# A fused decoder block: the first weight block's low half on VectorE, ScalarE and VectorE in another order in the head, and four powers of the queries' norms behind the state-space units on GpSimd

## The chip, the core and the metric

One Trainium2 chip, one core of it. The metric is the device time of one execution in microseconds (us), lower is better. The kernel is one program with five engines, each of which works through its own instruction list in order: TensorE (PE; its weight loads are counted apart as PEld), VectorE (DVE), ScalarE (ACT), GpSimd (POOL) and SyncE (SP, which here only issues transfers).

## The reference

One decoder layer over 512 tokens of width 1024, all float32, with three token mixers side by side: a sparse attention that picks its keys with an indexer (DSA), an attention with compressed, selected and windowed keys (NSA), and a state-space mixer in chunks of 128 tokens (SSD).

```python
h = rms_norm(x, g1)
u = h @ W_in                      # 1024 x D_in, split among the three mixers and three gates
y_A = DSA(u_A) @ W_br_A
y_B = NSA(u_B) @ W_br_B           # its queries are RMS-normed per head of 64
y_C = SSD(u_C) @ W_br_C
x = x + (sig(g_A)*y_A + sig(g_B)*y_B + sig(g_C)*y_C) @ W_out
x = x + relu(rms_norm(x, g2) @ W_1)**2 @ W_2

def rms_norm(x, g):
    return x * lax.rsqrt(jnp.mean(x*x, axis=-1, keepdims=True) + EPS) * g
```

## The kernel before, in words

**Products.** Each float32 product is made of three matmuls on numbers split into a high and a low part: `whi`·`hTh` (L459), `wlo`·`hTh` (L460) and `whi`·`hTl` (L461). `hTh` and `hTl` are the split, normed and transposed input; `whi` and `wlo` the split weights.

**The weight stream.** An object `ws` loads raw blocks of weights (`wraw`, three buffers, issued by SP) and splits them: ScalarE copies the high part (L173), then the difference is the low part (L175), on VectorE, or on GpSimd for the blocks whose number is in the set `LOWP`. Before the change, block 0 is in that set.

**The head.** The 512 tokens are four blocks of 128, x0 to x3 (in the lists of instructions x0 is `x_121`, x1 `x_124`, x2 `x_125`, x3 `x_126`). x0 takes a path of its own: it is transposed, multiplied by the gain `g1c` per column (`xg`, L406, two halves), then by `rb` (L432), the reciprocal root of each token laid along a row by a small matmul on `dg` (L416), and split into `hTh` (ScalarE, L433) and `hTl` (VectorE, L434). The blocks x1 to x3 are squared and summed on ScalarE (L394, L396), get a root on GpSimd (a power, L410), are scaled in place by VectorE (two L413 of 512 columns each), transposed by TensorE into `pT` (L428, eight 128x128 for each block), and split by ScalarE (`hTh`, L438) and VectorE (`hTl`, L439). `pT` has two buffers of four transposes each, so that the transposes of one block need the buffers that the block ahead of it left: both its `hTh` and its `hTl` must have read them. The first projection, 96 matmuls of 456 columns, goes over four weight blocks (0 to 3), two column halves of each and the four token blocks.

Small constants are loaded on SP between the weight blocks: `gq_d`, `gk_d`, `gk_n` (L324, read by VectorE in L344 and L345) and, later, `dsk` (read in L357 into `dcol`).

**The state-space mixer** runs through the middle of the kernel, its units woven between the matmuls of later projections. For each unit GpSimd masks `E` (L1345), ScalarE takes exponentials of it (L1348), VectorE multiplies (L1355), TensorE multiplies with `xt` and `hst`, VectorE and GpSimd combine (`eab`, L1366, L1367), and the result is gated and squared (`zsl` and `yv`, L1387 to L1404).

**The NSA queries** lie as raw rows; the sums of squares of each head are in `ssn`. Four powers on GpSimd (L1812, one for each token block) make the reciprocal roots in `rs8`. Then GpSimd issues the loads of the queries back from memory (`qu`, L1046), and TensorE makes the scores (L1087).

**What sets the order.** The program is written in Python, and a scheduler with a model of the engines' timelines orders the instructions of all engines, each engine's list fixed when the kernel is built. `tc.high_priority(...)` raises a group, `with tc.issue_after(X):` lets an instruction be placed only after X. So an edit at one place can reorder others. Semaphores hold an instruction until what it reads is written, and until buffers that it writes are free.

Of the kernel before, what the change touches and what calls it, by code (L numbers as in the profile page):

```python
# [10 lines left out]
ALU = mybir.AluOpType  # L11
# [12 lines left out]
NS = 6  # L24
RAWB = 3
LEAD = 3
LOWP = {0} | set(range(8, 12)) | set(range(17, 24))
WE = 2
NH = 4
BH = 2  # L30
# [6 lines left out]
HB = {4: 2, 5: 3}  # L37
# [4 lines left out]
def build_kernel(ctx, tc, A, out):  # L42
    nc = tc.nc
    pe, act, dve, pool = nc.tensor, nc.scalar, nc.vector, nc.gpsimd
# [5 lines left out]
    def bc(ap, shape):  # L50
        return ap.to_broadcast(shape)
# [63 lines left out]
    xt = []  # L115
# [18 lines left out]
    class WS:  # L134
# [24 lines left out]
        def split(s):  # L159
            i = s.nsplit  # L160
            while s.nload <= i:
                s.load()
            _, n, w = s.specs[i]
            r = s.raw.pop(i)
            m = n * w
            after = None
            if callable(r):
                after = r.after
                r = r(False)
            hi = wp.tile([128, 1024], F32R, name="whi", tag="whi", bufs=NS)  # L170
            lo = wp.tile([128, 1024], F32R, name="wlo", tag="wlo", bufs=NS)
            with tc.issue_after(HX[HB[i]][0]) if i in HB else nullcontext():
                act.activation(hi[:, :m], r[:, :m], AF.Copy)  # L173
            with tc.issue_after(H0[0][1]) if i == 1 else nullcontext():
                (pool if i in LOWP else dve).tensor_tensor(lo[:, :m], r[:, :m], f(hi[:, :m]), op=ALU.subtract)  # L175
            s.hl[i] = (hi[:, :m].rearrange("p (a b) -> p a b", b=w), lo[:, :m].rearrange("p (a b) -> p a b", b=w))
            s.nsplit += 1
            if after is not None:
                after()
# [123 lines left out]
    for t in range(NB):  # L303
        if t:
            nc.sync.dma_start(xt[t], dram(A["x"], t * 128 * D, [[D, 128], [1, D]]))
        if t == 2:
            ws.split()
        for _ in range((2, 1, 1, 0)[t]):
            ws.load()

# [62 lines left out]
    sq_junk = x0.tile([128, D], mybir.dt.bfloat16, name="sq_junk")  # L373
    ss1 = cp.tile([128, NB], F32, name="ss1")
    rs1 = cp.tile([128, NB], F32, name="rs1")
    H0, XG, g1p = [], [], []
    HX = {}
    wm = ps("pv", [128, 512])

    def warm(n, ref=None):  # L380
        with tc.issue_after(getattr(ref, "ins", ref)) if ref is not None else nullcontext():
            for _ in range(n):
                pe.matmul(wm[:, 0:128], ident, ident, start=True, stop=True)
# [6 lines left out]
    for t in range(NB):  # L390
        with tc.high_priority(offset=0 if t else HP):
            if t == 1:
                with tc.issue_after(H0[0][0]):
                    act.activation(sq_junk, xt[t], AF.Square, accum_out=ss1[:, t:t + 1])  # L394
            elif t:
                act.activation(sq_junk, xt[t], AF.Square, accum_out=ss1[:, t:t + 1])  # L396
            else:
                act.activation(sq_junk[:, 0:512], xt[0][:, 0:512], AF.Square, accum_out=ssh[:, 0:1])
                dve.tensor_tensor_reduce(xg, xt[0][:, 512:], xt[0][:, 512:], 1.0, 0.0, ALU.mult, ALU.add, accum_out=ssh[:, 1:2])
                dve.tensor_tensor(ss1[:, 0:1], ssh[:, 0:1], ssh[:, 1:2], op=ALU.add)  # L400
                for k0 in range(0, KT, 4):
                    p = ps("pT", [128, 4, 128])
                    for k in range(4):
                        i_ = pe.transpose(p[:, k], xt[t][:, (k0 + k) * 128:(k0 + k + 1) * 128], ident)
                    xg_ = x0.tile([128, 4, 128], F32, name=f"xg{k0}")
                    dve.tensor_tensor(xg_, p, bc(g1c[:, k0:k0 + 4, None], [128, 4, 128]), op=ALU.mult)  # L406
                    XG.append(xg_)
                warm(WARM[1], i_)
            dve.tensor_scalar(ss1[:, t:t + 1], ss1[:, t:t + 1], 1.0 / D, EPS, op0=ALU.mult, op1=ALU.add)
            pool.tensor_tensor(rs1[:, t:t + 1], ss1[:, t:t + 1], mhalf[:, :1], op=ALU.pow)  # L410
            if t:
                for i, c in enumerate((0, 512)):
                    dve.scalar_tensor_tensor(xt[t][:, c:c + 512], xt[t][:, c:c + 512], rs1[:, t:t + 1], g1p[i], op0=ALU.mult, op1=ALU.mult)  # L413
            else:
                dg = x0.tile([128, 128], F32, name="dg")
                dve.tensor_scalar(dg, ident, rs1[:, 0:1], None, op0=ALU.mult)  # L416
                rb = ps("pF", [128, 512])[:, 0:128]
                i_ = pe.matmul(rb, ones, dg, start=True, stop=True)
                for c in (0, 512):
                    p = ps("sc", [128, 512])  # L420
                    with tc.issue_after(getattr(i_, "ins", i_)):
                        pe.matmul(p, one1, g1w[:, c:c + 512], start=True, stop=True)
                    g1p.append(p)
            for k0 in range(0, KT, 4):
                if t:
                    p = ps("pT", [128, 4, 128])
                    for k in range(4):
                        pe.transpose(p[:, k], xt[t][:, (k0 + k) * 128:(k0 + k + 1) * 128], ident)  # L428
                else:
                    hsl = (slice(None), slice(k0, k0 + 4), slice(0, 128))  # L430
                    xg_ = XG[k0 // 4]
                    dve.tensor_tensor(xg_, xg_, bc(rb[:, None, :], [128, 4, 128]), op=ALU.mult)  # L432
                    h0 = act.activation(hTh[hsl], xg_, AF.Copy)  # L433
                    l0 = dve.tensor_tensor(hTl[hsl], xg_, f(hTh[hsl]), op=ALU.subtract)  # L434
                    H0.append([getattr(i, "ins", i) for i in (h0, l0)])
                    continue
                hsl = (slice(None), slice(k0, k0 + 4), slice(t * 128, t * 128 + 128))
                i_ = act.activation(hTh[hsl], p, AF.Copy)  # L438
                l_ = dve.tensor_tensor(hTl[hsl], p, f(hTh[hsl]), op=ALU.subtract)  # L439
                HX[t] = [getattr(v, "ins", v) for v in (i_, l_)]  # L440
# [436 lines left out]
            defer(1, tr)  # L877


    MASK = {}  # L880
    RIDX = R0

# [424 lines left out]
    def ssd(sv, ratio):  # L1307
# [50 lines left out]
        def stage3(u):  # L1358
            g, c = u.g, u.c
            py = ps("sc", [128, 512])  # L1360
            if c:
                po = ps("sc", [128, 512])
                for k in range(4):
                    mm(po[:, 128 * k:128 * k + 128], hst[g][:, 128 * k:128 * k + 128], u.b[:, 1])
                t1 = u.ea.rearrange("p k i -> p (k i)")
                dve.tensor_tensor(t1, po, t1, op=ALU.mult)  # L1366
                pool.tensor_tensor(t1, t1, u.xd, op=ALU.add)  # L1367
                yield ratio * 960
            if c < 3:
                pst = ps("pT", [128, 512])  # L1370
# [420 lines left out]
    def main():  # L1791
# [17 lines left out]
        yield "nq"  # L1809
        dve.tensor_scalar(ssn, ssn, 1.0, 64 * EPS, op0=ALU.mult, op1=ALU.add)  # L1810
        for b in dict.fromkeys(b for b, _ in NORD):
            pool.tensor_tensor(rs8[:, b, 16:32], ssn[:, b], mhalf[:, :16], op=ALU.pow)  # L1812
        at = popen("att", side="right")
        tail()
        yield from pipeline(nsa_units(R2), R2)
# [64 lines left out]
```

## Time and profile before

| | |
|---|---|
| runs | 1347.91, 1351.69, 1347.1 us, median 1347.91 |
| the profiled execution, its own time | 1345.58 us |
| its span (first to last instruction) | 1343.9 us |
| TensorE busy | 1326.1 us, 99% |
| VectorE, ScalarE, GpSimd busy | 994.2, 729.3, 266.8 us |
| mean granted TensorE clock | 0.997 |

The busy times are those of the one profiled execution and are shares of its span; 1.7 us of its time lie outside the span. Engines overlap, so their times don't add up to it. Matmuls are pipelined: a matmul's row gives more than its spacing (0.37 us for a spacing of 0.21 in the head).

### The profile page before, as it was taken

How to read it: one execution, taken by the hardware profiler on the slowest of the kernel's cores; microseconds unless marked ns; L12 is line 12 of the kernel's file. 1: busy time of each engine (PE TensorE's matmuls, PEld its weight loads, DVE VectorE, ACT ScalarE, POOL GpSimd, SP SyncE). 2: the span in 40 equal slices, each digit the busy share in tenths (PEclk: the TensorE clock that was granted, in tenths of full speed). 3: DMA queues.
4: the chain of work that ended last, by engine and by line, in shares of the span. 5: the costliest groups of instructions: out<-in, count | busy, mean ns of one | idle time of the engine just before them, and what ended most of it. 6: DMA issues, size and time to landing. Idle time of an engine off the chain costs nothing.

```text
span 1343.9 us, 19617 instructions
## 1 busy us (share of the span) xinstructions
PE 1326.1 (99%) x6827; PEld 1106.5 (82%) x6827; DVE 994.2 (74%) x1979; ACT 729.3 (54%) x1395; POOL 266.8 (20%) x236
## 2 busy tenths in 40 slices
PE   9999999999999999999999999999999999999998
PEld 7888788888887867888888888878889888888887
DVE  6499986889969576677687799978654766757841
ACT  5455336677768765565666656565343443444520
POOL 2225111111017677300000023213000201102000
PEclk9999999999999999999999999999999999999999
DMA  6436664464469899743344555334526646746431
GB/s 201 122 92 168 189 180 122 129 171 130 139 211 352 267 300 291 214 128 106 113 126 143 161 148 155 125 124 147 180 81 187 137 146 140 180 116 125 146 124 47
DMA packets 251777, 213.74 MB, mean 159 GB/s; under 512 B 15881, under 2 KB 203165, under 8 KB 251678
## 3 DMA queue, kind: packets, MB, share of 16 engines
q1 hardware_dynamic: 235708, 188.88, 46.5%
q0 software_dynamic: 15232, 20.98, 8.3%
q10 hardware_dynamic: 738, 2.63, 0.6%
q8 instruction: 54, 0.88, 0.3%
q14 instruction: 45, 0.37, 0.1%
HBM read 171.75 MB, written 40.70 MB: 158 GB/s over the span
## 4 chain that ended last, share of the span: by engine, by line
PE 82%; DVE 9%; DMA 4%; issue 2%; ACT 1%; POOL 1%; SPq 0%; DVEq 0%; POOLq 0%; ACTq 0%
PE pj L459 19%; PE pj L460 19%; PE pj L461 19%; PE sc L459 4%; PE sc L460 4%; PE sc L461 4%; PE pT L987 3%; PE pv L1000 2%; PE pv L999 2%; PE sc L927 2%; PE sc L928 2%; PE sc L1315 1%; DMA wraw<-in_w_in_dram 1%; DVE wlo L175 1%; DVE mask L904 1%
## 5 line engine op out<-in xcount | busy, mean ns | idle before, releaser
L173 ACT ACTIVATE whi<-wraw 128x1024 fp32r<-128x1024 f32 (+2 forms) x190 | 198.6, 1047 | 248.8 <-PE pj L460 123.7
L175 DVE TENSOR_TENSOR wlo<-wraw,whi 128x1024 fp32r<-128x1024 f32 (+1 forms) x178 | 222.8, 1254 | 99.5 <-ACT whi L173 98.7
L459 PE MATMUL pj<-hTh,whi 128*128 128x512 f32 x512 | 203.2, 397 | 4.4 <-DVE zo L736 2.3
L460 PE MATMUL pj<-hTl,whi 128*128 128x512 f32 x512 | 202.4, 395 | 0.0
L461 PE MATMUL pj<-hTh,wlo 128*128 128x512 f32 x512 | 202.1, 395 | 0.0
L936 ACT ACTIVATE p<-p,nb,rs 128x384 f32<-128x384 f32 (+3 forms) x160 | 107.8, 677 | 40.2 <-DVE nb L934 37.3
L459 PEld LDWEIGHTS pj<-hTh,whi 128*128 128x128 f32 x512 | 96.3, 188 | 23.6 <-DVE zo L736 2.7
L461 PEld LDWEIGHTS pj<-hTh,wlo 128*128 128x128 f32 x512 | 96.2, 188 | 19.0 <-issue 0.2
L460 PEld LDWEIGHTS pj<-hTl,whi 128*128 128x128 f32 x512 | 96.3, 188 | 18.2 <-issue 0.3
L460 PE MATMUL pj<-h2l,whi 128*128 128x512 f32 (+1 forms) x256 | 96.3, 376 | 0.0
L461 PE MATMUL pj<-h2h,wlo 128*128 128x512 f32 (+1 forms) x256 | 96.2, 376 | 0.0
L459 PE MATMUL pj<-h2h,whi 128*128 128x512 f32 (+1 forms) x256 | 96.1, 376 | 0.0
L459 PE MATMUL pj<-whi,hTh 128*128 128x512 f32 (+2 forms) x208 | 81.1, 390 | 0.6 <-ACT hTh L433 0.6
L461 PE MATMUL pj<-whi,hTl 128*128 128x512 f32 (+2 forms) x208 | 81.0, 389 | 0.0
L1046 POOL DMA_DIRECT2D qu<-q_d x32 | 23.5, 736 | 287.3 <-PE sc L928 121.3
L460 PE MATMUL pj<-wlo,hTh 128*128 128x512 f32 (+2 forms) x208 | 80.4, 387 | 0.0
L991 ACT ACTIVATE pth<-pT 128x512 fp32r<-128x512 f32 x92 | 53.1, 594 | 30.8 <-PE pT L987 29.9
L459 PE MATMUL sc<-whi,fh 128*128 128x512 f32 x168 | 65.4, 389 | 0.0
L460 PE MATMUL sc<-wlo,fh 128*128 128x512 f32 x168 | 65.4, 389 | 0.0
L461 PE MATMUL sc<-whi,fo 128*128 128x512 f32 x168 | 65.2, 389 | 0.0
L992 DVE TENSOR_TENSOR ptl<-pT,pth 128x512 fp32r<-128x512 f32 x92 | 61.6, 679 | 2.4 <-ACT pth L991 2.4
L987 PE MATMUL pT<-ident,p 128*128 128x128 f32 x368 | 63.1, 272 | 0.0
(431 smaller groups left out, 3275.5 us busy)
## 6 DMA issues: line engine op xcount, KB each, us to landing
wraw<-in_w_in_dram SPq DMA_DIRECT2D x84, 512.0 KB, 4.1
wraw<-in_w_ff_dram SPq DMA_DIRECT2D x58, 512.0 KB, 4.0
qd<-in_w_ff_dram POOLq DMA_DIRECT2D x18, 512.0 KB, 5.9
gld<-g_d SPq DMA_DIRECT2D x35, 256.0 KB, 2.6
q_d<-qev SPq DMA_DIRECT2D x64, 128.0 KB, 3.3
qu<-q_d POOLq DMA_DIRECT2D x32, 256.0 KB, 3.6
E<-ac_d SPq DMA_DIRECT2D x16, 512.0 KB, 6.1
xz<-xzt_d SPq DMA_DIRECT2D x16, 512.0 KB, 5.6
```

The lines of the kernel that those rows point to most:

```text
L173: act.activation(hi[:, :m], r[:, :m], AF.Copy)
L175: (pool if i in LOWP else dve).tensor_tensor(lo[:, :m], r[:, :m], f(hi[:, :m]), op=ALU.subtract)
L459: pe.matmul(o, lh, rh, start=first, stop=False)
L460: pe.matmul(o, lh, rl, start=False, stop=False)
L461: pe.matmul(o, ll, rh, start=False, stop=last)
L927: pe.matmul(s_[:, h % w, :n], u.q[h], kh[:, :n], start=True, stop=False)
L928: pe.matmul(s_[:, h % w, :n], u.q[h], kl[:, :n], start=False, stop=True)
L936: act.activation(u.p[h][:, :n], u.p[h][:, :n], AF.Exp, bias=u.nb[:, h:h + 1], scale=rs8[:, u.b, u.h0 + h:u.h0 + h + 1], accum_out=u.sm[:, ...
L987: pe.transpose(pt[:, h], u.p[h][:, kb * 128:kb * 128 + 128], ident)
L991: act.activation(ph, ptf, AF.Copy)
L992: dve.tensor_tensor(pl, ptf, f(ph), op=ALU.subtract)
L999: pe.matmul(o, vk, ph0, start=st, stop=False)
```

## The change

It has two parts.

In the head: block 0 leaves `LOWP`, so its low part goes to VectorE; the split of block 0 is issued after the first `xg`·`rb` rather than while x is loaded; VectorE's order is fixed as the first `xg`, then `dg`, and the low part of block 0 after the first multiplication by `rb`; ScalarE splits block 1 after the first `hTh` and block 2 after the second, and squares x1 after the second; the scaling of x1 (L413) comes after the second `hTl`.

In the middle: the four powers L1812 come after the last `eab` addition (L1367) of the state-space units.

```diff
-LOWP = {0} | set(range(8, 12)) | set(range(17, 24))
+LOWP = set(range(8, 12)) | set(range(17, 24))
...
-            with tc.issue_after(HX[HB[i]][0]) if i in HB else nullcontext():
+            with tc.issue_after(H0[0][0] if i == 1 else H0[1][0] if i == 2 else HX[HB[i]][0]) if i in (1, 2) or i in HB else nullcontext():
                 act.activation(hi[:, :m], r[:, :m], AF.Copy)
-            with tc.issue_after(H0[0][1]) if i == 1 else nullcontext():
+            with tc.issue_after(H0[0][1] if i else GX[2]) if i < 2 else nullcontext():
                 (pool if i in LOWP else dve).tensor_tensor(lo[:, :m], r[:, :m], f(hi[:, :m]), op=ALU.subtract)
...
-        if t == 2:
-            ws.split()
...
             if t == 1:
-                with tc.issue_after(H0[0][0]):
+                with tc.issue_after(H0[1][0]):
                     act.activation(sq_junk, xt[t], AF.Square, accum_out=ss1[:, t:t + 1])
...
-                    dve.scalar_tensor_tensor(xt[t][:, c:c + 512], xt[t][:, c:c + 512], rs1[:, t:t + 1], g1p[i], op0=ALU.mult, op1=ALU.mult)
+                    with tc.issue_after(H0[1][1]) if t == 1 else nullcontext():
+                        dve.scalar_tensor_tensor(xt[t][:, c:c + 512], xt[t][:, c:c + 512], rs1[:, t:t + 1], g1p[i], op0=ALU.mult, op1=ALU.mult)
             else:
                 dg = x0.tile([128, 128], F32, name="dg")
-                dve.tensor_scalar(dg, ident, rs1[:, 0:1], None, op0=ALU.mult)
+                with tc.issue_after(GX[0]):
+                    dve.tensor_scalar(dg, ident, rs1[:, 0:1], None, op0=ALU.mult)
...
-                    dve.tensor_tensor(xg_, xg_, bc(rb[:, None, :], [128, 4, 128]), op=ALU.mult)
+                    v_ = dve.tensor_tensor(xg_, xg_, bc(rb[:, None, :], [128, 4, 128]), op=ALU.mult)
+                    GX.append(getattr(v_, "ins", v_))
+                    if k0 == 0:
+                        ws.split()
...
-                pool.tensor_tensor(t1, t1, u.xd, op=ALU.add)
+                v_ = pool.tensor_tensor(t1, t1, u.xd, op=ALU.add)
+                PL[0] = getattr(v_, "ins", v_)
...
-            pool.tensor_tensor(rs8[:, b, 16:32], ssn[:, b], mhalf[:, :16], op=ALU.pow)
+            with tc.issue_after(PL[0]):
+                pool.tensor_tensor(rs8[:, b, 16:32], ssn[:, b], mhalf[:, :16], op=ALU.pow)
```

(`GX` holds the four multiplications of `xg` in order, `H0` the pairs of `hTh` and `hTl` of x0.) In the lists below the lines of the changed kernel count a little higher: L413 is still the scaling, L428 has become L429, L439 L443, L459 to L461 L463 to L465, L1367 L1372, L1812 L1819, L1046 L1051.

VectorE in the head, before. x_124 is x1, x_125 x2, x_126 x3; `ss` belongs to the square sums:

```order
L175 TENSOR_TENSOR wlo<-wraw,whi 128x912
L409 TENSOR_SCALAR ss_167<-ss_167 128x1
L344 TENSOR_TENSOR g_dsa<-gq_d,gk_d 128x64
L345 TENSOR_TENSOR g_nsa<-gk_n,gq_n 128x192
L409 TENSOR_SCALAR ss_167<-ss_167 128x1
L439 TENSOR_TENSOR hTl<-pT,hTh 128x4x128 x2
L413 SCALAR_TENSOR_TENSOR x_125<-x_125,rs_168,sc 128x512 x2
L413 SCALAR_TENSOR_TENSOR x_126<-x_126,rs_168,sc 128x512 x2
L175 TENSOR_TENSOR wlo<-wraw,whi 128x912
L357 TENSOR_SCALAR dcol<-dsk 64x16 x2
L439 TENSOR_TENSOR hTl<-pT,hTh 128x4x128 x2
```

Here the two `hTl` of x1 stand ahead of the scalings of x2 and x3. VectorE at the same place, after:

```order
L342 TENSOR_TENSOR g_dsa<-gq_d,gk_d 128x64
L175 TENSOR_TENSOR wlo<-wraw,whi 128x912
L413 SCALAR_TENSOR_TENSOR x_124<-x_124,rs_164,sc 128x512 x2
L343 TENSOR_TENSOR g_nsa<-gk_n,gq_n 128x192
L408 TENSOR_SCALAR ss_163<-ss_163 128x1 x2
L175 TENSOR_TENSOR wlo<-wraw,whi 128x912
L413 SCALAR_TENSOR_TENSOR x_125<-x_125,rs_164,sc 128x512 x2
L355 TENSOR_SCALAR dcol<-dsk 64x16 x2
L413 SCALAR_TENSOR_TENSOR x_126<-x_126,rs_164,sc 128x512 x2
L443 TENSOR_TENSOR hTl<-pT,hTh 128x4x128 x4
```

The low part of block 3 (the second L175), the scalings of x2 and x3 and `dcol` have moved ahead of x1's `hTl`, and `g_dsa` ahead of the low part of block 2. TensorE in the head, after, from the transposes of x1 on:

```order
L429 MATMUL pT<-ident,x_124 128x128 x8
L463 MATMUL pj<-whi,hTh 128x456 x2
L464 MATMUL pj<-wlo,hTh 128x456 x2
L465 MATMUL pj<-whi,hTl 128x456
L463 MATMUL pj<-whi,hTh 128x456
L464 MATMUL pj<-wlo,hTh 128x456
L465 MATMUL pj<-whi,hTl 128x456
L429 MATMUL pT<-ident,x_125 128x128 x4
L465 MATMUL pj<-whi,hTl 128x456
```

After, 18 matmuls of the projection stand ahead of the transposes of x1, and 8 more, those of this list, ahead of the first transposes of x2: 26. Before, it was 13 and 25: 38 ahead of the transposes of x2.

GpSimd at the end of the state-space units, before:

```order
L1403 TENSOR_TENSOR yv<-yv 128x256
L1812 TENSOR_TENSOR rs_316<-ssn,mhalf 128x16 x4
L1404 TENSOR_TENSOR sq_4351<-sq_4351,yv 128x256
L1376 TENSOR_TENSOR hst<-hst,sv_dec 128x512
L1367 TENSOR_TENSOR eab<-eab,xz 128x512
L1350 TENSOR_TENSOR xt<-xs,sv_dth 128x512
L1367 TENSOR_TENSOR eab<-eab,xz 128x512
L1345 AFFINE_SELECT E<-E 128x1024
L1403 TENSOR_TENSOR yv<-yv 128x256
L1404 TENSOR_TENSOR sq_4351<-sq_4351,yv 128x256
L1367 TENSOR_TENSOR eab<-eab,xz 128x512
L1046 DMA qu<-q_d_1_66 128x2x256 x2
```

And after:

```order
L1355 TENSOR_TENSOR xt<-xs,sv_dth 128x512
L1350 AFFINE_SELECT E<-E 128x1024
L1409 TENSOR_TENSOR yv<-yv 128x256
L1410 TENSOR_TENSOR sq_4351<-sq_4351,yv 128x256
L1372 TENSOR_TENSOR eab<-eab,xz 128x512 x2
L1819 TENSOR_TENSOR rs_316<-ssn,mhalf 128x16 x4
L1051 DMA qu<-q_d_1_66 128x2x256 x2
```

The four powers have moved past the last units and stand right ahead of the loads of the queries. From there on the NSA attention and the output projections are in another order on all engines; between the head and this place the lists are the same as before.

More of the change, by code (lines that the diff above doesn't have):

```diff
@@ L375, in build_kernel @@
     rs1 = cp.tile([128, NB], F32, name="rs1")
-    H0, XG, g1p = [], [], []
+    H0, XG, GX, g1p = [], [], [], []
     HX = {}
@@ L405, in build_kernel @@
                     xg_ = x0.tile([128, 4, 128], F32, name=f"xg{k0}")
-                    dve.tensor_tensor(xg_, p, bc(g1c[:, k0:k0 + 4, None], [128, 4, 128]), op=ALU.mult)
+                    v_ = dve.tensor_tensor(xg_, p, bc(g1c[:, k0:k0 + 4, None], [128, 4, 128]), op=ALU.mult)
                     XG.append(xg_)
+                    GX.append(getattr(v_, "ins", v_))
                 warm(WARM[1], i_)
@@ L431, in build_kernel @@
                     xg_ = XG[k0 // 4]
-                    dve.tensor_tensor(xg_, xg_, bc(rb[:, None, :], [128, 4, 128]), op=ALU.mult)
+                    v_ = dve.tensor_tensor(xg_, xg_, bc(rb[:, None, :], [128, 4, 128]), op=ALU.mult)
+                    GX.append(getattr(v_, "ins", v_))
+                    if k0 == 0:
+                        ws.split()
                     h0 = act.activation(hTh[hsl], xg_, AF.Copy)
@@ L877, in conv @@
             defer(1, tr)
+    PL = [None]
     MASK = {}
```

## The prediction

> **What bounds the kernel now.** I read the page first: the busy times, and the shares of the chain that ended last.
>
> ```profile
> PE 1326.1 (99%) x6827; PEld 1106.5 (82%) x6827; DVE 994.2 (74%) x1979; ACT 729.3 (54%) x1395; POOL 266.8 (20%) x236
> PE 82%; DVE 9%; DMA 4%; issue 2%; ACT 1%; POOL 1%; SPq 0%; DVEq 0%; POOLq 0%; ACTq 0%
> ```
>
> TensorE is busy all but 17.8 us of the 1343.9, so the change can win only where TensorE idles or runs at a lower clock. The second view was what TensorE waited for, in all, times, longest. These are the waits at the edited places.
>
> ```profile
> PE pj L459 <- ACT hTh L433: 0.6, 1, 0.6
> PE pT L1442 <- DVE sk L1429: 0.6, 1, 0.6
> PE pv L1315 <- issue: 0.3, 1, 0.3
> PE pj L459 <- ACT E L1348: 1.9, 1, 1.9
> ```
>
> The first is that of the projection's first matmul: the head can win 0.6 us there; the next two lie in the middle, which can win 0.6 + 0.3 = 0.9 us; the last is a wait for the state-space units' exponentials. The third view was the table by stage (length, then busy time of TensorE, its weight loads, VectorE, ScalarE, GpSimd, the granted clock, DMA share, GB/s), for the head, for a stall at 474.5 with the stretch behind it, and for the attention at the end.
>
> ```profile
> 10.00:20.00 10.00, 10.00 (x45) 8.71 (x45) 9.55 (x18) 6.25 (x12) 2.18 (x3) 0.84 0.72 244
> 474.50:477.10 2.60, 0.34 (x3) 0.04 (x1) 2.60 (x4) 1.01 (x2) 2.21 (x2) 1.00 1.09 334
> 477.10:481.00 3.90, 3.90 (x13) 3.19 (x14) 2.97 (x3) 3.30 (x11) 2.10 (x2) 0.56 1.13 327
> 20.00:30.00 10.00, 10.00 (x58) 9.10 (x57) 5.73 (x11) 5.82 (x16) 0.00 (x0) 1.00 0.40 130
> 840.00:880.00 40.00, 39.00 (x194) 32.21 (x193) 34.53 (x85) 23.70 (x51) 9.19 (x5) 1.00 0.39 124
> 880.00:920.00 40.00, 38.27 (x190) 30.63 (x189) 33.90 (x65) 22.90 (x42) 10.67 (x7) 1.00 0.43 135
> ```
>
> From 10 to 20 us TensorE never idles, but VectorE is 96% busy with 0.45 us left. That is the engine to which the change gives one more split. And a stall of 2.60 − 0.34 = 2.3 us is followed by a clock of 0.56 over 3.90 us: a second price of 3.90 × 0.44 = 1.7 us.
>
> **The head, part by part.** The timeline of before (start, length, engine) has the durations.
>
> ```profile
> 6.91 1.98 PE L422 MATMUL sc<-g1w,one 1*128 1x512 f32 x4
> 7.68 1.27 DVE L432 TENSOR_TENSOR xg<-xg,pF 128x512 f32<-128x512 f32 x2
> 7.80 2.13 POOL L175 TENSOR_TENSOR wlo<-wraw,whi 128x912 fp32r<-128x912 f32 x1 [1.75 <-ACT whi L173]
> 9.53 0.53 PE L459 MATMUL pj<-whi,hTh 128*128 128x456 f32 x1 [0.63 <-ACT hTh L433]
> 10.40 1.09 DVE L175 TENSOR_TENSOR wlo<-wraw,whi 128x912 fp32r<-128x912 f32 x1
> 11.48 0.67 DVE L434 TENSOR_TENSOR hTl<-xg,hTh 128x512 fp32r<-128x512 f32 x1
> ```
>
> *First matmul.* TensorE is done with L422 at 6.91 + 1.98 = 8.9; today it starts at 9.53. With ScalarE free for `hTh` at once, the most that is won is 0.6 us. But the gain is not kept: what follows needs VectorE. The low part of block 0 leaves GpSimd (2.13 us there) and costs VectorE 1.09. I lay VectorE's new list out with these durations: first multiplication by `rb` done at 7.68 + 0.64 = 8.3, low part of block 0 at 9.4, second multiplication 10.05, `hTl` 10.7, low part of block 1 11.8, `hTl` 12.5, and the mean of x1's squares 12.65 (0.15, its row stands with x1 below). Two later rows of the list read constants that come by DMA:
>
> ```profile
> 7.74 0.33 SPq L324 DMA_DIRECT2D gk_d<-in_dsa_k_norm_dram  x1
> gk_d<-in_dsa_k_norm_dram SPq DMA_DIRECT2D x1, 32.0 KB, 5.7
> 15.01 0.22 DVE L344 TENSOR_TENSOR g_dsa<-gq_d,gk_d 128x64 f32<-128x64 f32 x1
> L324 SPq DMA_DIRECT2D dsk<-in_ssd_d_dram x1: 429/429/429, 16.0 to 16.0; - x1
> DMA to landing us min/median/max: 4.2/4.2/4.2
> 20.32 0.34 DVE L357 TENSOR_SCALAR dcol<-dsk 64x16 f32<-64x16 f32 x2
> ```
>
> The load of `gk_d` (issue at 7.74, 5.7 us to landing) is there at 13.4. Today `g_dsa` is asked at 15.0 and waits for nothing; in the new list it stands ahead of the low part of block 2 and waits 0.8 us: 13.65. SP still issues both loads in the same place, after the second and around the third weight block.
>
> *x1.* The rest of the chain has these rows.
>
> ```profile
> 14.13 1.03 PE L428 MATMUL pT<-ident,x 128*128 128x128 f32 x8
> 14.77 1.09 ACT L438 ACTIVATE hTh<-pT 128x512 fp32r<-128x512 f32 x2 [0.52 <-PE pT L428]
> 14.94 0.15 DVE L409 TENSOR_SCALAR ss<-ss 128x1 f32<-128x1 f32 x1
> 15.14 0.36 DVE L345 TENSOR_TENSOR g_nsa<-gk_n,gq_n 128x192 f32<-128x192 f32 x1
> 15.47 1.28 DVE L439 TENSOR_TENSOR hTl<-pT,hTh 128x512 fp32r<-128x512 f32 x2
> 16.67 2.72 DVE L413 SCALAR_TENSOR_TENSOR x<-x,rs,sc 128x512 f32<-128x512 f32 x4
> 20.15 0.37 PE L459 MATMUL pj<-whi,hTh 128*128 128x456 f32 x1
> 20.36 1.03 PE L428 MATMUL pT<-ident,x 128*128 128x128 f32 x8
> ```
>
> Low part of block 2: 14.75. Scaling of x1 (half of 2.72): 16.1. Its transposes start 2 us later than the 14.13 of today, with 18 matmuls in front of them instead of 13.
>
> *x2, where the cost is.* `pT` has two buffers, and x1 fills both. The transposes of x2 overwrite the first once x1's first `hTl` has read it. Today that `hTl` starts at 15.47, ahead of the scalings of x2 and x3; the transposes of x2 at 20.36 wait for nothing (the row before them starts 0.21 earlier, the matmul spacing of this stretch). In the new list x1's `hTl` stands behind `g_nsa` and two means (0.36 + 0.3: 16.8), the low part of block 3 (17.9), the scaling of x2 (19.25), `dcol`, and the scaling of x3. `dcol` reads `dsk`, issued at 16.00 and 4.2 us on its way: 20.2, plus 0.34 is 20.55. The scaling of x3 ends at 21.9, the first `hTl` (half of 1.28) at 22.6. ScalarE's `hTh` (1.09 for both) is long done. So x2's transposes start at about 22.65, against 20.36 today.
>
> TensorE by then has done 26 matmuls of the projection, not 38: 12 × 0.21 = 2.5 us of work that is still ahead. The price of the head is 22.65 − 20.36 + 2.5 = **+4.8 us**. Its lower end leaves out the wait for `dsk`: 19.25 + 0.34 + 1.36 + 0.64 = 21.6, price +3.7. To cost nothing, the `hTl` would have to be done at 20.36 − 2.5 = 17.9. The 0.6 us of the first matmul lie inside these numbers, since they count from the transposes. TensorE's idle time there: the 18 matmuls end near 15.8, transposes to 17.1, 8 matmuls at 0.21 to 18.8, idle from 18.8 to 22.65: 3.9 us. Nothing behind it can hide it: by the busy time, TensorE has 1% free.
>
> *The clock.* The only row on what a stall of this length does is the one at 474.5: 2.3 us of it, then a clock of 0.56, price 1.7 us. The bounds are 0 and 1.7; a stall longer than that row's speaks for 1.7. I take **+1.7**.
>
> [...]
>
> **The middle.** GpSimd's rows at the end of the state-space units, behind two of TensorE's for the matmuls' spacing there (521.32 − 521.09 = 0.23):
>
> ```profile
> 521.09 0.39 PE L460 MATMUL pj<-hTl,whi 128*128 128x512 f32 x1
> 521.32 0.39 PE L461 MATMUL pj<-hTh,wlo 128*128 128x512 f32 x1
> 521.39 12.45 POOL L1812 TENSOR_TENSOR rs<-ssn,mhalf 128x16 f32<-128x16 f32 x4
> 544.36 1.30 POOL L1367 TENSOR_TENSOR eab<-eab,xz 128x512 f32<-128x512 f32 x1 [1.01 <-DVE eab L1366]
> 550.01 2.93 POOL L1046 DMA_DIRECT2D qu<-q_d  x4 [4.35 <-DVE zsl L1387]
> qu<-q_d POOLq DMA_DIRECT2D x32, 256.0 KB, 3.6
> ```
>
> The four powers hold GpSimd for 12.45 us ahead of nine of its state-space steps. Moved behind the last `eab`, those steps come up to 12.45 us sooner, so TensorE's two waits there (0.6 + 0.3) can go: −0.9 at best. What is queued behind the powers now is the loads of `qu`: if the units end the full 12.45 us sooner, the powers end where the last `eab` ends today, 544.36 + 1.30 = 545.7, ahead of the 550.0 at which the loads start today. In the new list TensorE has 81 matmuls between the last state-space product and the first scores (38 before), 81 × 0.23 = 18.6 us, which cover 12.45 + 3.6 = 16.1 us; with that cover gone, the scores would wait up to 16.1 − 38 × 0.23 = 7 us. But now the last state-space products follow each other more closely (1 matmul instead of 23 between the last-but-one unit's state product and the last unit's), so TensorE may wait there for the chain mask, exponentials, multiplication:
>
> ```profile
> 518.24 1.09 POOL L1345 TENSOR_SCALAR_AFFINE_SELECT E<-E 128x1024 f32<-128x1024 f32 x1 [1.54 <-ACT eab L1344]
> 520.45 2.44 ACT L1348 ACTIVATE E<-E,sv_nac 128x128 f32<-128x128 f32 x8
> ```
>
> Bounds of that new wait: 0, and the 1.9 us that TensorE waited in all for these exponentials. I take a third, +0.6, as the powers no longer stand ahead of the mask. Middle: −0.9 + 0.6 = **−0.3**, from −0.9 to +1.0.
>
> **The order from there on.** From 515 us all lists are shuffled. The stretch 840 to 920 has 80 − 39.00 − 38.27 = 2.7 us of idle TensorE; a new order may remove it or have as much again: 0, from −2.7 to +2.7.
>
> **Sum:** +4.8 + 1.7 − 0.3 = +6.2 against the profiled 1345.58: 1351.8. The median of the runs (1347.91) is 2.3 above the profiled execution, so I forecast 1347.91 + 6.2 = **1354**.
>
> **Rivals.** *The head late, the clock whole.* The sum without 1.7, or without the wait for `dsk` (1.1 less): 1347.91 + 4.5 = 1352.4, or with both 1351.3. The stall at 474.5 speaks against it.
>
> *Not slower: the later order gives it back.* The new order from 515 on wins both the 0.9 us of the middle and the 2.7 us of 840 to 920, and the clock stays whole: 4.8 − 0.9 − 2.7 = +1.2, so 1349.1. It decides once the later stages win 2.2 us or more (6.2 − 4.0). Those waits are ones that a schedule can remove; against it, no edit aims at them.
>
> *Faster: the head is not late.* If `x1`'s `hTl` came by 17.9, the head would cost 0 or win the 0.6; with the same gains behind, −0.6 − 0.9 − 2.7 = −4.2, 1343.7. The order of VectorE's list speaks against it: 2.72 + 1.1 us of work stand newly ahead of it.
>
> *Worse: the loads of `qu` uncovered.* If the units end no earlier, loads end up to 4 us later than the cover: 1354 + 4 = 1358.
>
> **How the numbers follow.** Forecast 0.47, head late with whole clock or without `dsk` 0.20 (half of it above the bound), not slower 0.18, faster 0.10, worse 0.05. This kernel's measurement can tell about 0.3% (4.0 us: 1343.9 to 1351.95) from no change. Slower: 0.47 + 0.05 and 0.10 of the second, less 0.04 for the lower tail of the forecast's own range (1350.5 to 1357): 0.58. Faster 0.10, same 0.32. The range, down to the low side of the not slower case (1349.1 less another 2) and up to the worse case: 1347 to 1358.
>
> **What would show it.** Right: TensorE idle 3 to 4 us once before 23 us, waiting with L429 for `hTl` L443; `dcol` starting at 20.2 or later with VectorE idle ahead of it; a granted clock below 0.9 in 20 to 30 us, where it is 1.00 now; x1's `hTl` at about 22; GpSimd's powers after the last `eab`, and no TensorE wait by L1442. Wrong: x2's transposes by 20 us, or TensorE idle time behind 515 us that differs by over 3 us from before.

## The result and the profile after

The changed kernel takes 1362.5 us in the median of 6 runs (1359.47 to 1363.43), before takes 1350.61 beside it (6 runs, 1347.1 to 1353.03): ratio 1.009, interval 1.0073 to 1.0106, slower by 11.9 us. In a second series (below) the ratio was 1.0056, 1.0037 to 1.0074. The profiled execution took 1359.47 us, its span is 1357.8, 13.9 more than before's. I had forecast 1354, slower by 6.2, in a range of 1347 to 1358: the sign was right, the size too small, and the time lies above the range.

The page of the changed kernel, busy times and the chain's shares:

```profile
PE 1330.7 (98%) x6827; PEld 1107.2 (82%) x6827; DVE 994.6 (73%) x1980; ACT 727.7 (54%) x1395; POOL 259.3 (19%) x235
PE 78%; DVE 10%; DMA 7%; issue 2%; ACT 2%; POOL 1%; SPq 1%; DVEq 0%; POOLq 0%; ACTq 0%
```

TensorE's idle time rose from 17.8 us to 1357.8 − 1330.7 = 27.1. The view of what TensorE waited for names where (total, times, longest):

```profile
PE pT L429 <- DVE hTl L443: 5.2, 1, 5.2
PE pj L464 <- DVE wlo L175: 1.7, 1, 1.7
PE pT L1448 <- DVE sk L1435: 1.2, 1, 1.2
PE sc L1320 <- DVE yv L1390: 1.1, 1, 1.1
PE sc L1092 <- issue: 0.8, 1, 0.8
```

The first row is the wait that was forecast, transposes of x2 for x1's low part, with 5.2 us instead of 3.9. The table by stage, in the same columns as before's:

```profile
10.00:20.00 10.00, 7.66 (x33) 5.90 (x32) 7.18 (x14) 6.07 (x12) 2.56 (x3) 0.89 0.69 220
20.00:30.00 10.00, 5.38 (x19) 4.84 (x20) 3.64 (x7) 1.33 (x5) 0.00 (x0) 0.66 0.28 103
```

Before had TensorE busy for all of these 20 us. VectorE, 96% busy in the first ten of them before, is now busy 72% and then 36%: it stands and waits, as its timeline shows (an arrow names the idle time ahead and what ended it):

```profile
14.01 0.23 DVE L342 TENSOR_TENSOR g_dsa<-gq_d,gk_d 128x64 f32<-128x64 f32 x1 [2.29 <-DMA gk_d<-in_dsa_k_norm_dram]
14.16 1.10 DVE L175 TENSOR_TENSOR wlo<-wraw,whi 128x912 fp32r<-128x912 f32 x1
15.18 1.40 DVE L413 SCALAR_TENSOR_TENSOR x<-x,rs,sc 128x512 f32<-128x512 f32 x2
16.96 1.11 DVE L175 TENSOR_TENSOR wlo<-wraw,whi 128x912 fp32r<-128x912 f32 x1
18.51 1.41 DVE L413 SCALAR_TENSOR_TENSOR x<-x,rs,sc 128x512 f32<-128x512 f32 x2 [0.44 <-POOL rs L409]
22.19 0.35 DVE L355 TENSOR_SCALAR dcol<-dsk 64x16 f32<-64x16 f32 x2 [2.27 <-DMA dsk<-in_ssd_d_dram]
22.55 1.41 DVE L413 SCALAR_TENSOR_TENSOR x<-x,rs,sc 128x512 f32<-128x512 f32 x2
23.88 1.28 DVE L443 TENSOR_TENSOR hTl<-pT,hTh 128x512 fp32r<-128x512 f32 x2
```

Two 0.2-us instructions that read late constants, `g_dsa` and `dcol`, hold it for 2.3 us each, and x1's low part stands behind both. TensorE at the same place, before the transposes and at them:

```profile
19.08 0.37 PE L465 MATMUL pj<-whi,hTl 128*128 128x456 f32 x1
24.62 1.11 PE L429 MATMUL pT<-ident,x 128*128 128x128 f32 x4 [5.17 <-DVE hTl L443]
25.38 0.73 PE L465 MATMUL pj<-whi,hTl 128*128 128x456 f32 x1
```

SyncE's rows of the changed kernel and, in the next fence, of before show why `dsk` is later:

```profile
12.23 1.67 SPq L154 DMA_DIRECT2D wraw<-in_w_in_dram  x2
15.13 0.52 SPq L154 DMA_DIRECT2D wraw<-in_w_in_dram  x1
16.67 0.43 SPq L322 DMA_DIRECT2D dsk<-in_ssd_d_dram  x1
```

```profile
10.38 0.89 SPq L154 DMA_DIRECT2D wraw<-in_w_in_dram  x2
13.85 0.39 SPq L154 DMA_DIRECT2D wraw<-in_w_in_dram  x1
16.00 0.43 SPq L324 DMA_DIRECT2D dsk<-in_ssd_d_dram  x1
```

The fourth weight block (two loads, `x2`) is issued 1.85 us later, behind two small loads (`rows`) that have moved ahead of it, and the fifth (`x1`) 1.28 later; `dsk` is issued 0.67 us later than before's 16.00, and reaches VectorE 22.19 − 16.67 = 5.5 us after that, where before it took 4.2.

In the middle, GpSimd has the powers behind the last `eab` as written, and the loads of `qu` right after them, at 561.13 where they were at 550.01:

```profile
547.70 1.31 POOL L1372 TENSOR_TENSOR eab<-eab,xz 128x512 f32<-128x512 f32 x1 [5.16 <-DVE eab L1371]
548.96 12.22 POOL L1819 TENSOR_TENSOR rs<-ssn,mhalf 128x16 f32<-128x16 f32 x4
561.13 2.93 POOL L1051 DMA_DIRECT2D qu<-q_d  x4
```

**Where the 13.9 us lie.** TensorE issues the same number of matmuls in all kernels here, so the start of its k-th matmul in two traces can be set against each other. The table gives lengths in us between the 1st, 131st, 2701st (515 us in before), 3001st, 4301st, 4951st matmul and the last; "before" is the trace of the prediction, the other rows belong to the experiments below. Behind 515 us the kernels with moved powers run in another order than those without, so their columns there are compared as stretches, not matmul by matmul. The expectations below speak of the 200th matmul; the differences between the kernels there are those of the head column to 0.1 us.

| trace | head, to 131 | to 2701 | to 3001 | to 4301 | to 4951 | to the last |
|---|---|---|---|---|---|---|
| before | 28.7 | 484.4 | 55.7 | 249.6 | 126.4 | 393.0 |
| before, second trace | 28.8 | 483.9 | 60.0 | 249.6 | 130.6 | 393.0 |
| after | 37.6 | 484.4 | 58.8 | 249.1 | 128.8 | 393.0 |
| after, second trace | 38.2 | 484.1 | 60.1 | 249.1 | 129.3 | 393.0 |
| head alone | 38.5 | 484.6 | 57.6 | 250.1 | 130.0 | 393.0 |
| powers alone | 28.7 | 482.7 | 60.1 | 249.1 | 129.9 | 393.0 |
| after, `dcol` late | 32.9 | 484.5 | 61.9 | 249.1 | 130.6 | 393.0 |
| after, block 0 on GpSimd | 29.1 | 482.4 | 60.4 | 249.1 | 129.6 | 393.0 |
| mended head | 31.1 | 484.6 | 56.8 | 249.6 | 128.4 | 393.0 |
| mended head, second | 31.3 | 482.2 | 57.9 | 250.0 | 129.4 | 393.0 |
| before, block 0 on VectorE | 31.2 | 485.3 | 60.2 | 249.6 | 127.7 | 393.0 |

The head is longer by 8.9 and 9.5 us in the two traces of the changed kernel, and up to 515 us nothing of this is given back. What happens to it later these traces can't tell: the two stretches behind 515 us are what differs most between two executions of the *same* kernel: before's second trace has 4.3 and 4.2 us more in them than the trace from which I predicted.

### The profile page after: what moved, and what is told of

It reads as the page before. It is cut to its first block, busy times and chain, and to the rows that moved or that the text cites. A ratio compares the mean times of both kernels' runs of the same rounds, so it can differ in the third digit from the quotient of the medians.

```text
span 1357.8 us, 19624 instructions
## 1 busy us (share of the span) xinstructions
PE 1330.7 (98%) x6827; PEld 1107.2 (82%) x6827; DVE 994.6 (73%) x1980; ACT 727.7 (54%) x1395; POOL 259.3 (19%) x235
## 4 chain that ended last, share of the span: by engine, by line
PE 78%; DVE 10%; DMA 7%; issue 2%; ACT 2%; POOL 1%; SPq 1%; DVEq 0%; POOLq 0%; ACTq 0%
PE pj L463 18%; PE pj L465 18%; PE pj L464 18%; PE sc L464 3%; PE sc L463 3%; PE sc L465 3%; PE pT L992 3%; PE pv L1005 2%; PE pv L1004 2%; DMA wraw<-in_w_in_dram 2%; PE sc L933 2%; PE sc L932 2%; DMA q_d<-qev 1%; DVE mask L909 1%; DVE wlo L175 1%
## 5 line engine op out<-in xcount | busy, mean ns | idle before, releaser
L175 DVE TENSOR_TENSOR wlo<-wraw,whi 128x1024 fp32r<-128x1024 f32 (+1 forms) x179 | 224.0, 1254 | 104.4 <-ACT whi L173 103.4
L463 PE MATMUL pj<-hTh,whi 128*128 128x512 f32 x512 | 203.7, 398 | 3.7 <-ACT E L1353 1.9
L465 PE MATMUL pj<-hTh,wlo 128*128 128x512 f32 x512 | 203.3, 397 | 0.0
L463 PEld LDWEIGHTS pj<-hTh,whi 128*128 128x128 f32 x512 | 96.6, 189 | 22.8 <-ACT E L1353 2.1
L465 PEld LDWEIGHTS pj<-hTh,wlo 128*128 128x128 f32 x512 | 96.7, 189 | 19.1 <-issue 0.5
L465 PE MATMUL pj<-h2h,wlo 128*128 128x512 f32 (+1 forms) x256 | 96.2, 376 | 0.0
L463 PE MATMUL pj<-h2h,whi 128*128 128x512 f32 (+1 forms) x256 | 96.1, 376 | 0.0
L463 PE MATMUL pj<-whi,hTh 128*128 128x512 f32 (+2 forms) x208 | 81.6, 392 | 0.1
L465 PE MATMUL pj<-whi,hTl 128*128 128x512 f32 (+2 forms) x208 | 81.1, 390 | 0.0
L1051 POOL DMA_DIRECT2D qu<-q_d x32 | 23.5, 735 | 295.3 <-PE sc L933 145.7
L997 DVE TENSOR_TENSOR ptl<-pT,pth 128x512 fp32r<-128x512 f32 x92 | 61.9, 680 | 6.0 <-ACT pth L996 6.0
L463 PE MATMUL sc<-whi,fh 128*128 128x512 f32 x168 | 65.4, 389 | 0.0
L465 PE MATMUL sc<-whi,fo 128*128 128x512 f32 x168 | 65.2, 389 | 0.0
```

What stands on the lines that cost most here:

```text
L463: pe.matmul(o, lh, rh, start=first, stop=False)
L465: pe.matmul(o, ll, rh, start=False, stop=last)
L997: dve.tensor_tensor(pl, ptf, f(ph), op=ALU.subtract)
```

## The experiments

**The two kernels once more.** No edit.

> The changed kernel once more, beside runs of before on the same chip, for what no single trace tells: how much of the +13.9 us between the two spans and of the +11.9 between the two medians is the change. Theory A (the parts add: head alone +5.8, powers alone +1.5 by their intervals on one chip): 6 to 8 us slower than before (1.0045 to 1.006). Theory C (the parts strengthen each other, late head and new order together): 11 to 13 us (1.008 to 1.010). In the trace, whatever the total: TensorE waits 5 us for x1's low part, and the 200th matmul is 8 to 10 us later than in before's trace.

> The kernel before once more, for a second trace of it. Theory D (the trace that I predicted from, 1345.58 us, was one of the shortest executions, since few half-clock stretches and little DMA delay fell into it): head the same within 0.2 us up to the 200th matmul, but 3 to 8 us more behind it, with other stalls followed by a half clock than the one at 474.5. Rival (executions differ by the head's DMA landings): the 200th matmul differs by over 1 us.

Measured: the changed kernel 1361.09 (11 runs) against 1352.65 (22 runs of before), medians 8.4 us apart; ratio 1.0056, 1.0037 to 1.0074, or 5.0 to 10.0 us. The ratio lies in Theory A's range, and the interval leaves out Theory C's 11 to 13. The first series gave 9.9 to 14.3 us; the two intervals only just meet, near 10, so the change's size is not known better than 5 to 14 us. In the second trace of the changed kernel TensorE waits 4.9 us for x1's low part. The second trace of before took 1353.55 us, 8.0 more than the one I predicted from; its head is the same to 0.1 us, and the difference lies behind 515: Theory D. The waits of that second trace behind 500 us:

```profile
PE pT L1442 <- DVE sk L1429: 2.3, 2, 1.6
PE pv L1315 <- PE pj L459: 1.0, 1, 1.0
PE pF L619 <- DVE qev L623: 0.8, 1, 0.8
```

The wait for `sk`, 0.6 in the first trace, was 2.3 here, with nothing changed, and a granted clock of 0.50 from 535.72 to 539.13 followed it. So the 5.5 us that the single pair of traces laid on the change behind 515 us (58.8 + 128.8 against 55.7 + 126.4) can't be told from the spread between executions of one kernel.

**The head alone.** Powers as before; from 515 us on this kernel has before's order.

```diff
-            with tc.issue_after(PL[0]):
-                pool.tensor_tensor(rs8[:, b, 16:32], ssn[:, b], mhalf[:, :16], op=ALU.pow)
+            pool.tensor_tensor(rs8[:, b, 16:32], ssn[:, b], mhalf[:, :16], op=ALU.pow)
```

> The head's part of the change alone; the four powers stay where they were before, and with them the order of everything behind 515 us is that of before. Theory A (the loss is made of two pieces that add: the head's stall with its half clock, +8.9 us by the changed kernel's trace at its 200th matmul, and the new order behind 515 us, about +5): first projection 8.9 us later than before, the whole 8 to 10 us slower than before (1.006 to 1.007), TensorE waiting 5.2 us for x1's low part. Theory B (the head's delay is partly taken up later, as in the DVE-bound stretch from 70 us, and the order behind 515 carries most): 3 to 6 us slower.

**The powers alone.** Before, with the two edits at L1367 and L1812 of the change and nothing else.

> The four powers behind the last eab addition alone; the head is that of before. Theory A: no difference up to 515 us, then +3 us between 520 and 600 (new waits ahead of the last state-space products and of the first scores) and +2 us in 840 to 960: 4 to 6 us slower (1.003 to 1.0045). Theory B' (the trace's +5 behind 515 us is a shift of phases that the late head brings, and the order itself costs nothing): within 1 us of before. My forecast had -0.3 for this part.

Measured in one series: the head alone 1357.46 (6 runs), ratio 1.0043 (1.0027 to 1.0059), 3.7 to 8.0 us; the powers alone 1353.79 (10 runs), ratio 1.0011 (0.9999 to 1.0023), −0.1 to +3.1 us; before 1353.21 (27 runs). In the traces the head alone has its stretch of 38.5 us, and the powers alone the head of before to 0.0 us. The head carries most of the loss, but less than its trace's head shows: 9.8 us there, 5.8 by the ratio of the runs (the medians are 4.3 apart), and the interval ends where A's 8 to 10 us begin. B's 3 to 6 us fits; what takes the rest back is not shown, and up to 515 us the trace has given back nothing. For the powers A's 4 to 6 us did not hold; B′'s "within 1 us" fits the medians, but the interval reaches 3.1. The new waits that A counted are in the trace of the powers alone,

```profile
PE pT L1444 <- DVE sk L1431: 1.8, 1, 1.8
PE sc L1316 <- DVE yv L1386: 1.1, 1, 1.1
```

but the first of them is no larger than in before's second trace. Only the second, for a product of the last unit, is new in every kernel with moved powers.

**`dcol` after x1's low part.** The whole change; only two VectorE instructions move.

```diff
-            dve.tensor_scalar(dcol[r], CL["dsk"]...
+            with tc.issue_after(HX[1][1]):
+                dve.tensor_scalar(dcol[r], CL["dsk"]...
```

> The whole change, but the two dcol instructions, which wait for the load of dsk, come after x1's second low part; no other instruction moves on TensorE, ScalarE, GpSimd and SP. Theory A (VectorE stands 2.3 us at dsk with x3's scaling and x1's low part behind it, and TensorE's 5.2 us hang on that): x2's transposes start at 21.9 instead of 24.6, TensorE's wait there falls to about 2.5, the clock still halves once, the whole is 2.5 to 3 us faster than the changed kernel. Rival (the transposes wait for ScalarE's high part or for a buffer in another way): same wait of 5.2 us, same time as the changed kernel.

Its VectorE and TensorE at the place:

```profile
18.67 2.72 DVE L414 SCALAR_TENSOR_TENSOR x<-x,rs,sc 128x512 f32<-128x512 f32 x4
21.30 1.28 DVE L444 TENSOR_TENSOR hTl<-pT,hTh 128x512 fp32r<-128x512 f32 x2
22.50 0.34 DVE L356 TENSOR_SCALAR dcol<-dsk 64x16 f32<-64x16 f32 x2
22.04 0.66 PE L430 MATMUL pT<-ident,x 128*128 128x128 f32 x4 [1.94 <-DVE hTl L444]
```

Measured: 1359.19 (10 runs), ratio to before 1.0033 (1.0018 to 1.0049), against the changed kernel's 1.0056 in another series; the two intervals overlap, so the runs alone don't show the gain, and the trace has to. The transposes start at 22.04 (21.9 expected) instead of 24.62, the wait falls from 5.2 to 1.9, and the head from 37.6 to 32.9 us. That is 4.7 us for two instructions of 0.17 us each: 2.6 by the earlier transposes, and the other 2.1 is the second price, since the clock stays whole here (1.00 from 17.49 to 27.72), against my expectation. The rival is out.

**Block 0 back on GpSimd.** The whole change but one number.

```diff
-LOWP = set(range(8, 12)) | set(range(17, 24))
+LOWP = {0} | set(range(8, 12)) | set(range(17, 24))
```

> The whole change, but the low part of weight block 0 goes back to GpSimd. VectorE then has x1's first low part ahead of the scaling of x2, and 41 matmuls stand ahead of x2's transposes. Theory A (one more split on VectorE is what tips the scheduler's order, and the order is what costs): no wait for x1's low part over 0.5 us, the first projection within 1 us of before (or up to 0.6 us earlier), the whole 4 to 6 us slower than before for the powers alone. Rival (the new pins on ScalarE and on x1's scaling cost by themselves): first projection still 3 us or more late.

Its VectorE has x1's low part in two halves around the scaling of x2, and `dcol` behind both:

```profile
15.75 0.68 DVE L443 TENSOR_TENSOR hTl<-pT,hTh 128x512 fp32r<-128x512 f32 x1
17.97 1.40 DVE L413 SCALAR_TENSOR_TENSOR x<-x,rs,sc 128x512 f32<-128x512 f32 x2
19.29 0.68 DVE L443 TENSOR_TENSOR hTl<-pT,hTh 128x512 fp32r<-128x512 f32 x1
21.82 0.35 DVE L355 TENSOR_SCALAR dcol<-dsk 64x16 f32<-64x16 f32 x2 [0.54 <-DMA dsk<-in_ssd_d_dram]
20.80 1.03 PE L429 MATMUL pT<-ident,x 128*128 128x128 f32 x8
```

Measured: 1354.98 (10 runs), ratio 1.0015 (1.0000 to 1.0030), head 29.1 us, no wait at x2's transposes, which 38 matmuls precede (the expectation had counted 41). With one number set back, all the pins of the head (its new `issue_after` lines on ScalarE and VectorE) cost 0.4 us there. The head is as Theory A had it, the total is not: 4 to 6 us were expected, and it is 0 to 4.1, as the powers alone give. `dsk` lands late here too, at 21.8, but nothing that TensorE needs stands behind it.

**The one number alone**, on before:

> Before with one edit alone: block 0 leaves LOWP, so that VectorE makes its low part; none of the pins, powers as before. VectorE's list now has x1's first low part between the scalings of x2 and x3, the fourth weight block is loaded earlier, and 31 matmuls (12 on each of the blocks 0 and 1, 7 more) stand ahead of x2's transposes instead of 38. Theory A (the place of x1's first low part sets the stall): x2's transposes at 19 to 20.5, a wait of 0 to 2 us, the 200th matmul within +2 us of before, total within 4 us of before. Rival (the split on VectorE alone makes most of the changed kernel's +9): the 200th matmul 4 us or more late.

```profile
19.80 0.66 PE L428 MATMUL pT<-ident,x 128*128 128x128 f32 x4 [0.62 <-DVE hTl L439]
```

Measured: 1355.02 (10 runs), ratio 1.0027 (1.0009 to 1.0044), head 31.2 us, 2.5 more than in before; the wait was inside Theory A's range, the head 0.5 us past it (26 matmuls stand ahead of x2's transposes in the trace, not 31). Of the 2.5, 1.1 is there from the start: without the pins VectorE makes block 0's low part ahead of the multiplications by `rb`, and the first matmul starts at 10.67 instead of 9.53. So neither half of the head's edits makes the loss of 8.9 alone: the pins cost 0.4, the split 2.5, and together they make the order in which `dcol` stands ahead of x1's low part.

**The head mended.** The whole head with block 0 on VectorE, powers as before; the readers of late constants and the scalings of x2 and x3 come after x1's second low part.

```diff
-        dve.tensor_tensor(g_dsa, CL["gq_d"], ...
+        with tc.issue_after(HX[1][1]):
+            dve.tensor_tensor(g_dsa, CL["gq_d"], ...
...                                   # g_nsa and dcol likewise
-                    with tc.issue_after(H0[1][1]) if t == 1 else nullcontext():
+                    with tc.issue_after(H0[1][1] if t == 1 else HX[1][1]):
```

> The head's part of the change with its VectorE order mended (powers as before): g_dsa, g_nsa and dcol, the readers of the late constants, come after x1's second low part, and so do the scalings of x2 and x3; the low part of block 0 stays on VectorE. Theory A (the order alone costs, not the added 1.1 us split): VectorE is never held by a constant, x2's transposes stand behind 45 matmuls and start near 22, no TensorE wait over 1 us after the first matmul, the 200th matmul within 1 us of before, total within 3 us of before (0.998 to 1.002). Rival (VectorE simply has no room for the split, 96% busy from 10 to 20 us): the 200th matmul at least 2.5 us late, total 2 us or more slower.

Measured: 1352.8 (12 runs), ratio 1.0001 (0.9982 to 1.0021): no difference to before in the runs, as Theory A had it, though the interval (−2.4 to +2.8 us) can't exclude the rival's 2. In the trace the head is 31.1 us, 2.4 more than before's, which is next to the rival's 2.5 and not A's 1, and x2's transposes start at 24.01 behind 47 matmuls, not near 22 behind 45. Before has one half-clock stretch in the head (0.50 from 9.79 to 13.20); here TensorE waits 0.6 us for x0's first low part, and a second stretch follows, put at 1.6 us in the next expectation.

**The head mended once more.** The low part of block 0 after the second multiplication by `rb`, and the small loads behind `gk_n` after the fourth weight block:

```diff
-                    if k0 == 0:
+                    if k0 == 4:
                         ws.split()
...
-            with tc.issue_after(H0[0][1] if i else GX[2]) if i < 2 else nullcontext():
+            with tc.issue_after(H0[0][1] if i else GX[3]) if i < 2 else nullcontext():
...
-            nc.sync.dma_start(t, dram(ap, 0, ...
+            with tc.issue_after(ws.l3) if rows or n == 32 else nullcontext():
+                nc.sync.dma_start(t, dram(ap, 0, ...
```

> The mended head of the last experiment with two more places put right: the low part of block 0 comes after the second multiplication by rb (so that x0's first low part no longer leaves TensorE idle for 0.65 us in the half-clock stretch), and the small constants behind gk_n are loaded after the fourth weight block; the powers as before. Theory E (what was left of the mended head's +2.4 us is that 0.65 us idle and the second half-clock stretch of 1.6 us that followed it, not a lack of room on VectorE): one half-clock stretch in the head as in before, the 200th matmul 0 to 0.7 us earlier than in before's trace, total within 3 us of before, with the sign open. Rival (VectorE has no room for the split): the 200th matmul still 1 us or more late.

```profile
16.06 0.96 ACT L175 ACTIVATE whi<-wraw 128x912 fp32r<-128x912 f32 x1 [1.56 <-DMA wraw<-in_w_in_dram]
17.05 1.11 DVE L177 TENSOR_TENSOR wlo<-wraw,whi 128x912 fp32r<-128x912 f32 x1 [1.84 <-ACT whi L175]
17.07 0.48 PE L469 MATMUL pj<-whi,hTh 128*128 128x456 f32 x1 [0.64 <-ACT whi L175]
18.21 0.47 PE L470 MATMUL pj<-wlo,hTh 128*128 128x456 f32 x1 [0.67 <-DVE wlo L177]
```

Measured: 1354.21 (12 runs), ratio 1.0026 (1.0010 to 1.0041), head 31.3 us. Theory E fell: there is one half-clock stretch again (a mean clock of 0.66 from 10 to 15 us, 0.68 in before, and 1.00 from 15 on), and the head is no shorter. What TensorE now waits for is the fourth weight block's halves (0.64 + 0.67 us), which its list asks for behind x1's transposes. Up to the end of those transposes this head is level with before's, to 0.1 us; the two waits set it back by 1.7 us from start to start, and most of the rest, 0.8, comes around the transposes of x2 and x3. At the fourth block VectorE is not what is short: it stands 1.84 us for the high part, and ScalarE 1.56 for the load. Whether the split has room in some order stays open: with it on VectorE, and x1's low part not behind `dcol`, the head was 2.4 to 2.6 us longer than before in three orders, and 4.2 in the change with `dcol` late.

No version here is shown to beat the kernel before.

## Why the prediction was right and where it failed

- **First matmul.** Earlier, and worth nothing: 9.05 instead of 9.53, and behind it TensorE waited 1.7 us for block 2's low part, which stood behind `g_dsa` and its wait for `gk_d`. `g_dsa` was forecast to end at 13.65; it started at 14.01, since `gk_d` was issued 0.44 us later than in before. This cost x1 little: its transposes began at 16.45, where I had 16.1.
- **x1's low part behind `dcol` and two scalings.** The mechanism was right to the instruction. Moving `dcol` alone took 4.7 of the head's 8.9 us away, and setting the split back took all but 0.4.
- **The step that failed is the landing of `dsk`.** I wrote that SP still issues both loads in the same place (in before's rows `gk_d` stands behind the third weight block's loads and `dsk` behind the fifth's), and took issue and way, 16.00 + 4.2 = 20.2, from the trace of before. `dcol` started at 22.19: `dsk` was issued 0.67 us later, behind weight loads that small loads left out of my sum had pushed back, and the way took 5.5 us instead of 4.2. So the transposes began at 24.62, not 22.65: the term of the head was 24.62 − 20.36 + 2.5 = 6.8 where I had 4.8. My lower bound left the wait out altogether; an upper one, with a later landing, was missing.
- **Why the way was longer** stays open, but the fourth block's place is not the reason. With block 0 back on GpSimd that block is loaded at 10.61, almost as early as in before, and `dsk`, issued at 16.24, lands at 21.80 all the same, 5.6 us later. What that trace shares with the changed kernel is the fifth block's load 1.54 us ahead of `dsk`, as in the changed kernel's second trace and in head alone, where `dcol` starts 5.7 and 6.1 us after the issue. In before, in its second trace and in powers alone that load is 2.1 us ahead, and the way takes 4.2, 4.1 and 4.4. No run moves it alone.
- **The clock.** +1.7 was forecast. The ten matmuls from 25.38 to 28.95, most of them 0.38 us apart instead of 0.21, took 3.9 us against 2.15 with `dcol` late, 1.8 more, and the four transposes ahead of them 0.3 more (0.76 against 0.42). So 6.8 + 1.8 + 0.3 = 8.9 accounts for the head. The size was nearly right; the row that I took it from says less than I read in it, since stalls near 2 us went with either clock: the 2.3 us at 474.5 with 0.50 from 477.42 on, the 1.9 us with `dcol` late with 1.00. The 5.2 us in the changed kernel went with 0.50 from 22.41 to 29.23.
- **The middle and the order behind.** −0.3 and 0 were forecast; the powers alone measured −0.1 to +3.1 us. The wait for `sk` at L1442 did not go (1.2 in the changed kernel, 1.8 with the powers alone), so the 0.9 us that I meant to win were not won. The last `eab` ended 6.5 us sooner with the powers alone (539.15 against 545.66; 1.7 of this was there at 515 already), not the full 12.45: ahead of it GpSimd waited 7.0 us for VectorE's `eab`.
- **The base.** The forecast stood on the median of three runs, 1347.91. Before's medians in the later series were 1350.61, 1353.21, 1352.65 and 1351.59. Of the 8.5 us between 1354 and 1362.5, 2.7 are this, 2.4 the head's terms (8.9 for 6.5), and 3.4 I can lay to no term: executions of one kernel differ by more than that behind 515 us, and in the second series the medians are 8.4 apart, no more than the head's 8.9. So the head's 2.4 alone would have left the time inside the range (1356.4); the range had no room for the base either.

The rivals: the clock was not whole in the head, no trace shows the later order giving the loss back, and the head was late. "Worse" had the first scores wait for the loads of `qu`; TensorE idles 0.8 us there (L1092), and the view names nothing that it waits for.

## What to carry to other kernels

In an in-order engine's list, a tiny instruction that reads a late load can hold up the whole chain behind it, here 4.7 us for two instructions of 0.17: find such readers first, and keep them behind work that others wait for. When a list moves, redo the landing time of every load from the new list of the issuing queue, since the change may move it: here the landing copied from the old trace came 2 us later, though no edit named the load. Before trusting a difference between two single traces, take a second trace of the kernel before: here it differed from the first by 8 us, all of it away from the edit.

## What the runs showed of the hardware

In the traces of before and of after the granted clock is 1.00 or 0.50. Up to 1340 us it is 0.50 from 9.79 to 13.20 and from 477.42 to 480.83 in before, and from 8.75 to 12.17, 22.41 to 29.23 and 414.94 to 418.35 in after: for 3.41 us, once for 6.82, and within a trace the starts lie whole multiples of 3.413 us apart (137 of them in before, 4 and 115 in after). I cut each trace into cells of 3.41 us from these starts. Behind the first stretch, the cells ahead of a half clock are those in which TensorE was busy least, rather than those with the longest stall: in before a wait of 2.28 us for `zo`, up to 150.29, went with 1.00, one of 2.26 us for `qev`, up to 477.06, with 0.50. Rows of the table by stage, each a cell and the next one, of before (the first pair of lines, then a second pair), of powers alone, and of after:

```profile
146.31:149.72 3.41, 1.70 (x8) 1.08 (x6) 3.27 (x9) 1.54 (x2) 0.00 (x0) 1.00 0.34 77
149.72:153.13 3.41, 2.83 (x12) 2.36 (x13) 3.34 (x7) 0.00 (x0) 0.00 (x0) 1.00 0.75 187
474.00:477.42 3.42, 1.16 (x6) 0.68 (x7) 3.42 (x4) 1.30 (x3) 2.71 (x2) 1.00 1.03 323
477.42:480.83 3.41, 3.41 (x11) 2.74 (x10) 2.65 (x3) 2.83 (x9) 2.10 (x2) 0.50 1.14 325
```

```profile
532.22:535.63 3.41, 1.66 (x11) 1.16 (x9) 1.66 (x6) 0.00 (x0) 0.00 (x0) 1.00 0.29 108
535.63:539.04 3.41, 3.41 (x21) 2.43 (x20) 3.31 (x4) 0.63 (x1) 1.16 (x1) 0.50 0.32 55
```

```profile
411.53:414.94 3.41, 1.48 (x19) 1.10 (x16) 3.12 (x5) 3.37 (x10) 3.12 (x3) 1.00 1.07 381
414.94:418.35 3.41, 3.41 (x9) 2.64 (x9) 3.41 (x4) 3.41 (x8) 1.48 (x2) 0.50 1.07 393
```

Of the cells at full clock between the first stretch and 1340 us in these traces of before and after, three had TensorE busy for less than 1.5 us (1.16 in before, 0.46 and 1.48 in after), and 0.50 followed each of them; behind all others, with 1.66 us or more, the clock was 1.00. In powers alone 0.50 followed a cell with 1.66 us, so these busy times alone do not tell which clock follows:

| cell | TensorE busy, us | clock of the next cell |
|---|---|---|
| after, 12.17 | 1.66 | 1.00 |
| powers alone, 532.22 | 1.66 | 0.50 |
| before, 146.31 | 1.70 | 1.00 |

At the start of the head low busy time is not what goes with it: both traces have their first half-clock stretch there, in before from 9.79 us behind a cell with TensorE busy for 2.78 us, in after from 8.75 us behind one with 3.04. Why is not shown.

The same wait for `E`, 1.9 us in before and in after, fell across two cells in before (2.16 us busy from 402.29 to 405.70, 2.72 from 405.70 to 409.11, and 1.00 in both and behind them), and inside one cell in after (1.48 us busy from 411.53), where 3.41 us at 0.50 followed, 1.7 us again. A stall of 3.9 us, as forecast for the head, leaves at most 3.41 − 1.95 = 1.46 us of work in one of two cells if it is cut in equal halves, and less in one of them if it is not; that is below the 1.48 us behind which the clock halved, so I would expect a half clock wherever such a stall fell (an estimate from these rows).
